# A two-layer decoder trunk on one core: the mixers' elementwise work on VectorE alone, and two weight parts split before the experts' last sum

## The chip, the core and the metric

One core of one Trainium2 chip. The metric is the device time of one execution in microseconds (us), as the median of several runs. TensorE does the matrix products, VectorE (DVE), ScalarE (ACT) and GpSimd (POOL) the elementwise work, SyncE (SP) issues the transfers from HBM.

## The reference, cut to what matters

T = 256 tokens of width 1024, two layers. Each layer has a mixer (three attention-like branches beside each other) and a mixture of 32 experts. All is float32.

```python
for l in range(2):
    mod = silu(c) @ ada_w[l] + ada_b[l]            # conditioning: 6 vectors of 1024
    sh1, sc1, gt1, sh2, sc2, gt2 = split(mod, 6)
    h = rms_norm(x, norm1_g[l]) * (1 + sc1) + sh1
    proj = h @ w_in[l]                             # 1024 -> 3524 columns
    rq, rk = rope(rq), rope(rk); ya = retention(rq, rk, rv, rg)
    yb = causal softmax attention with a cumulative forget gate (fq, fk, fv, ff)
    yc = causal softmax attention, low-rank q and kv, rope on 64 columns
    gates = sigmoid(h @ gate_w[l] + gate_b[l])     # 3 x 1024
    merged = g0 * (ya @ branch_w[0]) + g1 * (yb @ branch_w[1]) + g2 * (yc @ branch_w[2])
    x = x + gt1 * (merged @ out_w[l])
    h = rms_norm(x, norm2_g[l]) * (1 + sc2) + sh2
    x = x + gt2 * experts(h)                       # top-2 of 8 experts in the top group of 4
return rms_norm(x, final_g)
```

## The kernel before, in words

**Products in three parts.** The big products of the mixers run on TensorE as three cheaper ones (`mm3`, `gemm_tok`, `gemm_feat`). Weight and activation are each split into a high part, a cast to the type fp32r, and a low part, which is what the cast left over; high x high, high x low and low x high are added up in PSUM. A weight comes from HBM in tiles of 1 MiB (SP's queue, a ring of 12 slots, L141), and is consumed in chunks of 128 x 512. `split_w` (L247) makes the two parts of one chunk: ScalarE the high part (L256), VectorE or GpSimd the low part (L258), in one of four buffers `ws0` to `ws3`. `pump` (L242) is called once per chunk by the running product and keeps three chunks ready; it chooses the engine for the low part by a pattern: GpSimd, GpSimd, VectorE in general (`LO`), always GpSimd while `self.quiet` is set (`LO_HEADS`), which is the time of the softmax heads. An input slot is given back to the ring after its last low part.

**What runs between the chunks.** A product of eight chunks yields after each, and `step` then lets the generators in `live` go on by one step each: the heads of the two softmax attentions (L647 on, with the scaling L664), the forget gates (L804 to L820), the retention (scaling L908), and `chain`, the conditioning. `chain` takes its weights through VectorE: L505 and L507 multiply-add a 128 x 512 piece onto `acc`; TensorE sums `acc` over partitions and L525 adds the bias. So the order on each engine is that of the program text as these generators interleave; no engine reorders its own queue.

**Rotations and sums of branches.** `rope` (L632) makes four products on VectorE (L640 to L643) and the two sums on GpSimd (L644, L645). After a branch's product, `merge` multiplies with the gate on VectorE (L1146), and for the second and third branch `add_up` (L1117) adds the result to `merged` on GpSimd (L1120, 16 in all); for the last branch `split_a` then splits the sum for the output product (L268 on ScalarE, L269 on VectorE).

**The experts and the seam.** The experts' products take the weights unsplit, in 16 pairs; their elementwise work is VectorE's and ScalarE's. At the end `finish(n)` (L1368) adds the experts' sum to the residual for each half of the columns: L1375 and L1376 on VectorE, then a square with a sum of it on ScalarE (L1377), which writes its squares to `yp[n][0]` (`yh`). For n = 1 it comes after `open_split`, which opens the four buffers of the next layer. The next layer begins with `head` (L954): the norm, four warming matmuls, transposes, and, in its second piece, `split(2)` (L1003) for the first two chunks, with the low parts on GpSimd.

Of the kernel before, what the change touches and what calls it, by code (L numbers as in the profile page):

```python
# [8 lines left out]
F32 = mybir.dt.float32  # L9
# [4 lines left out]
AF = mybir.ActivationFunctionType  # L14
ALU = mybir.AluOpType
# [29 lines left out]
A_HG, A_MORE, A_HIDT, A_OH = (4864, 5888), (0, 2048, 6912), 4096, (4608, 8960)  # L45
# [7 lines left out]
ADA_LAG, ADA_DELAY = 5, 2  # L53

ADA_PAUSE = 4

LO_HEADS, LO = (1,), (0, 1, 1)

WAIT_MLA, WAIT_FOX, WAIT_RET, WAIT_PT = 4, 4, 2, 1
SLOTS = 12  # L60
# [107 lines left out]
class Trunk:  # L168
# [72 lines left out]

    def pump(self):  # L242
        while self.stream and len(self.splits) < len(self.ws) - 1:
            pattern = LO_HEADS if self.quiet else LO
            self.split_w(self.nc.gpsimd if pattern[(self.wsi + 1) % len(pattern)] else self.nc.vector)

    def split_w(self, eng):  # L247


        key, i, n, last = self.stream.popleft()  # L250
        if key not in self.held:
            self.held[key] = self.ring.take(key)
        w = self.held[key][1][:, i, :n]
        t = self.ws[self.wsi % len(self.ws)]
        hi, lo = t[:, 0, :n], t[:, 1, :n]
        self.nc.scalar.copy(hi, w)  # L256
        self.wsi += 1
        eng.tensor_tensor(lo, w, hi.bitcast(F32), ALU.subtract)  # L258
        self.splits.append((hi, lo))
        if last:  # L260
            self.ring.give(self.held.pop(key)[0])
# [370 lines left out]
    def rope(self, dst, src, t, heads):  # L632

        nc = self.nc
        b = self.v(A_ROPE, 2, heads, 32)
        c = self.cos[:, t][:, None, :].to_broadcast([P, heads, 32])
        s = self.sin[:, t][:, None, :].to_broadcast([P, heads, 32])
        x1, x2 = src[:, :, 0:32], src[:, :, 32:64]
        d1, d2 = dst[:, :, 0:32], dst[:, :, 32:64]
        nc.vector.tensor_tensor(b[:, 0], x2, s, ALU.mult)  # L640
        nc.vector.tensor_tensor(b[:, 1], x1, s, ALU.mult)
        nc.vector.tensor_tensor(d1, x1, c, ALU.mult)
        nc.vector.tensor_tensor(d2, x2, c, ALU.mult)  # L643
        nc.gpsimd.tensor_tensor(d1, d1, b[:, 0], ALU.subtract)  # L644
        nc.gpsimd.tensor_tensor(d2, d2, b[:, 1], ALU.add)  # L645

    def softmax_head(self, i, h, scores, bias, val, yr):  # L647

# [305 lines left out]
    def head(self, l):  # L954

        nc = self.nc
        xn = self.v(A_XN, 2, D)
        S, G = self.GS[:, 0, 0], self.GS[:, 0, 1]
        rs = [self.small(1) for _ in range(NT)]
        live = [self.inv_rms(t, rs[t]) for t in range(NT)]  # L960
        while live:
            self.step(live)
        for t in range(NT):
            nc.vector.tensor_scalar(xn[:, t, :512], self.x[:, t, :512], rs[t], None, ALU.mult)
            nc.scalar.mul(xn[:, t, 512:], self.x[:, t, 512:], rs[t])
        yield "normed"
        todo = []
        for g in range(2):
            for t in range(NT):
                ps = self.bank("s" if len(todo) < 3 and l else "g")  # L970
                for i in range(4):
                    j = 4 * g + i
                    self.tr(ps[:, 128 * i:128 * i + 128], xn[:, t, 128 * j:128 * j + 128])
                todo.append((g, t, ps))
        yield
        h32 = [self.v(A_H32 + 512 * k, 4, 128) for k in range(4)]

        def scaled(k):
            g, t, ps = todo[k]
            for i in range(4):  # L980
                j = 4 * g + i
                o, p = h32[k][:, i], ps[:, 128 * i:128 * i + 128]
                if t == 0:
                    nc.vector.tensor_scalar(o, p, G[:, j:j + 1], S[:, j:j + 1], ALU.mult, ALU.add)
                else:
                    nc.scalar.activation(o, p, AF.Identity, bias=S[:, j:j + 1], scale=G[:, j:j + 1])
            self.free(ps)

        def part(k, i):
            return self.hr[k // 2][:, i, :, 128 * (k % 2):128 * (k % 2) + 128]  # L990

        def high(k):
            nc.scalar.copy(part(k, 0), h32[k])

        def low(k):
            nc.vector.tensor_tensor(part(k, 1), h32[k], part(k, 0).bitcast(F32), ALU.subtract)

        def split(n):
            for _ in range(n):
                self.split_w(nc.gpsimd)  # L1000

        if l:
            split(2)  # L1003
        scaled(0)
        scaled(1)
        high(0)
        high(1)
        if l == 0:
            low(0)
            low(1)  # L1010
        yield
        if l == 0:
            split(2)
        scaled(2)
        if l:
            low(0)
            low(1)
        high(2)
        split(1)
        scaled(3)  # L1020
        low(2)
        high(3)
        low(3)
        split(1)

    def mixer(self, l):
        nc, run, finish = self.nc, self.run, self.finish
# [33 lines left out]
        ga = chain()  # L1061
        gh = self.heads.pop() if self.heads else self.head(l)
        if l:
            self.stream = deque(self.streams[l])
            next(gh)
            self.warm(4)
        self.together(gh)
# [46 lines left out]
        merged = self.v(A_MERGED, 8, 256)  # L1114
        sg = self.v(A_SG, 4, 256)

        def add_up(h, last):  # L1117
            for i in range(2):
                sl = slice(4 * h + 2 * i, 4 * h + 2 * i + 2)
                nc.gpsimd.tensor_tensor(merged[:, sl], merged[:, sl], sg[:, 2 * i:2 * i + 2], ALU.add)  # L1120
                yield
            for i in range(2 if last else 0):
                sl = slice(4 * h + 2 * i, 4 * h + 2 * i + 2)
                m = self.yr[1] if h == 0 else self.hr[0]
                self.split_a(m[:, 0, 2 * i:2 * i + 2], m[:, 1, 2 * i:2 * i + 2], merged[:, sl])
                yield
# [201 lines left out]
    def moe(self, l):  # L1328
        nc, tc = self.nc, self.tc
# [39 lines left out]
        def finish(n):  # L1369

            ns = slice(512 * n, 512 * n + 512)
            for t in range(NT):
                xs, ps = self.x[:, t, ns], self.sums[t][n]
                self.mm(ps, self.OT[:, 128 * t:128 * t + 128].bitcast(F32), y32[:, ns], False, True)
                nc.vector.tensor_tensor(hid, ps, self.gtb[:, ns], ALU.mult)  # L1375
                nc.vector.tensor_tensor(xs, xs, hid, ALU.add)  # L1376
                nc.scalar.activation(self.yp[n][0], xs, AF.Square, accum_out=self.ss[:, t, n:n + 1])  # L1377

        self.together(self.gather([self.v(A_OH[t], 2 * CAP) for t in range(NT)], hg[0], True))
        for p in range(NE // 2):  # L1380
# [242 lines left out]
```

## Time and profile before

| | |
|---|---|
| median of 3 runs | 1565.86 us (1561.02 to 1565.95) |
| the profiled execution | 1567.71 us, its span 1566.0 us |
| mixers, layer 0 and layer 1 | 0 to 335 us and 800 to 1095 us |
| experts, layer 0 and layer 1 | 335 to 800 us and 1095 us to the end |
| matmuls busy (PE) | 1488.0 us, 95% of the span |
| VectorE (DVE) | 641.0 us, 41% |
| ScalarE (ACT) | 449.8 us, 29% |
| GpSimd (POOL) | 336.6 us, 21%; 331.5 us of it in the mixers |
| mean granted TensorE clock | 0.973 |
| DMA | 342 GB/s over the span |

A share over the whole span mixes two kinds of stage. In the experts from 335 to 800 us VectorE is busy 103.9 us and GpSimd not at all; in the mixer from 0 to 335 they are busy 234.9 and 167.4 us. What matters in each stage is therefore read from views of that stage, and from the view that says for whom TensorE waited.

### The profile page before, as it was taken

Reading aid. Unit: us, or ns where it says so; the run is one execution under the profiler, and the core shown is the slowest. Engines: PE = TensorE matmul, PEld = TensorE weight load, DVE = VectorE, ACT = ScalarE, POOL = GpSimd, SP = SyncE. Lnnn points to the kernel's source line nnn. Section 1 sums busy time; section 2 is a strip of 40 time slices with the busy share of each in tenths; the row PEclk is TensorE's granted clock in tenths of the full one; section 3 lists DMA queues with packets and bytes.
Section 4 is the critical chain, followed back from the end, with each engine's and each line's share of the span. In section 5 each row is a group of like instructions: output and inputs, shape, how many; then the busy total and the mean of one; then the engine's idle time right before and its main releaser. Section 6 shows DMA issues by size and latency. Waiting matters only on the chain. (4 is left out here: it accounts for less than half of the span.)

```text
span 1566.0 us, 21356 instructions
## 1 busy us (share of the span) xinstructions
PE 1488.0 (95%) x8342; PEld 915.1 (58%) x8342; DVE 641.0 (41%) x1500; ACT 449.8 (29%) x896; POOL 336.6 (21%) x266
## 2 busy tenths in 40 slices
PE   6999999899999999999989999999999999999996
PEld 3877888654444444444458788896444444444442
DVE  3846878861222222122147559656222122222223
ACT  3555434331211111111154563353211111111111
POOL 1557546510000000000024664473000000000001
PEclk9899989899999999999999999999999999999998
DMA  9963676788999999999985646568899999999992
GB/s 385 367 236 135 231 280 243 295 348 361 421 421 421 420 421 421 421 419 421 410 336 188 228 176 251 209 230 314 353 421 421 420 421 422 421 420 419 421 416 108
DMA packets 78542, 535.16 MB, mean 342 GB/s; under 512 B 8608, under 2 KB 8864, under 8 KB 15968
## 3 DMA queue, kind: packets, MB, share of 16 engines
q1 hardware_dynamic: 77776, 532.89, 84.1%
q8 instruction: 69, 1.13, 0.3%
q10 hardware_dynamic: 656, 0.80, 0.1%
q14 instruction: 41, 0.34, 0.1%
HBM read 532.61 MB, written 1.05 MB: 341 GB/s over the span
## 5 line engine op out<-in xcount | busy, mean ns | idle before, releaser
L181 PE MATMUL bank<-slot,ar 128*64 128x512 f32 (+1 forms) x1880 | 491.4, 595 | 3.8 <-issue 1.6
L258 POOL TENSOR_TENSOR ws<-slot,ws 128x512 fp32r<-128x512 f32 (+1 forms) x209 | 284.4, 1372 | 711.8 <-ACT ws L256 693.6
L181 PEld LDWEIGHTS bank<-slot,ar 128*64 128x64 f32 (+1 forms) x1880 | 152.8, 138 | 276.8 <-issue 256.0
L256 ACT CAST ws<-slot 128x512 fp32r<-128x512 f32 (+1 forms) x276 | 169.3, 618 | 168.1 <-PE bank L181 154.3
L181 PE MATMUL bank<-hr,ws 128*128 128x256 f32 x1536 | 209.5, 296 | 7.7 <-POOL ws L258 6.7
L181 PE MATMUL bank<-ar 128*64 128x512 f32 (+3 forms) x692 | 209.3, 503 | 0.0
L181 PEld LDWEIGHTS bank<-hr,ws 128*128 128x128 f32 x1536 | 198.7, 201 | 13.7 <-POOL ws L258 7.3
L181 PE MATMUL bank<-ws,hr 128*128 128x512 f32 (+1 forms) x576 | 153.8, 413 | 9.1 <-DVE hr L269 4.3
L1325 ACT ACTIVATE ar<-bank,GS 128x128 f32<-128x128 f32 x128 | 58.5, 457 | 357.3 <-PE bank L181 326.6
L181 PE MATMUL bank<-more_left,ar 128*64 128x512 f32 x456 | 137.6, 595 | 0.0
L181 PEld LDWEIGHTS bank<-ar,x 128*128 128x128 f32 x1024 | 119.3, 192 | 25.1 <-issue 21.1
L507 DVE SCALAR_TENSOR_TENSOR acc<-slot,cz,acc 128x512 f32<-128x512 f32 x122 | 133.2, 1092 | 1.6
L181 PE MATMUL bank<-ar,x 128*128 128x128 f32 x1024 | 128.3, 279 | 1.8 <-DVE ar L1307 1.6
L181 PEld LDWEIGHTS bank<-ws,hr 128*128 128x128 f32 x576 | 108.7, 196 | 35.5 <-DVE hr L269 5.3
L1442 DVE SCALAR_TENSOR_TENSOR yl<-bank,wsl,yh 128x512 fp32r<-128x512 f32 x60 | 45.0, 751 | 157.1 <-ACT yh L1441 157.1
L181 PE MATMUL bank<-more_right,ar 128*64 128x512 f32 x308 | 106.4, 606 | 1.8 <-DMA more_left<-in_exp_w 1.8
L1359 DVE COPY wsl<-bank 64x1 f32<-64x1 f32 x64 | 10.0, 156 | 232.5 <-PE bank L181 232.1
L1560 POOL TENSOR_TENSOR ar<-x,cst 128x512 f32<-128x512 f32 x2 | 2.6, 1287 | 473.5 <-DVE x L1376 473.5
L1323 DVE TENSOR_SCALAR ar<-bank,GS 128x128 f32<-128x128 f32 x128 | 52.5, 410 | 116.3 <-ACT ar L1325 116.3
L258 DVE TENSOR_TENSOR ws<-slot,ws 128x512 fp32r<-128x512 f32 (+1 forms) x67 | 66.7, 997 | 70.8 <-ACT ws L256 65.4
L181 PEld LDWEIGHTS bank<-ar 128*64 128x64 f32 (+2 forms) x692 | 81.1, 155 | 24.6 <-issue 18.1
L1406 DVE TENSOR_TENSOR R<-R,bank 128x512 f32<-128x512 f32 x32 | 22.0, 687 | 178.4 <-PE bank L181 178.4
(244 smaller groups left out, 1362.2 us busy)
## 6 DMA issues: line engine op xcount, KB each, us to landing
slot<-in_exp_w SPq DMA_DIRECT2D x227, 1024.0 KB, 19.6
ar<-in_exp_w SPq DMA_DIRECT2D x54, 1024.0 KB, 19.8
more_left<-in_exp_w SPq DMA_DIRECT2D x54, 1024.0 KB, 19.8
slot<-in_ada_w SPq DMA_DIRECT2D x46, 1024.0 KB, 6.8
more_right<-in_exp_w SPq DMA_DIRECT2D x37, 1024.0 KB, 19.0
slot<-in_w_in SPq DMA_DIRECT2D x24, 1024.0 KB, 6.9
slot<-in_gate_w SPq DMA_DIRECT2D x23, 1024.0 KB, 5.3
slot<-in_branch_w SPq DMA_DIRECT2D x12, 1024.0 KB, 4.8
```

Of the source, the lines that this page charges most:

```text
L181: self.nc.tensor.matmul(out, lhsT, rhs, start=start, stop=stop, skip_group_check=True)
L256: self.nc.scalar.copy(hi, w)
L258: eng.tensor_tensor(lo, w, hi.bitcast(F32), ALU.subtract)
L507: nc.vector.scalar_tensor_tensor(acc, v[:, t, :], c, acc, ALU.mult, ALU.add)
L1323: nc.vector.tensor_scalar(hgT[:, j], pv[:, i], G[:, j:j + 1], S[:, j:j + 1], ALU.mult, ALU.add)
L1325: nc.scalar.activation(hgT[:, j], pv[:, i], AF.Identity, bias=S[:, j:j + 1], scale=G[:, j:j + 1])
L1359: nc.vector.tensor_copy(wsl(p)[es], ps[es, 256 + e:257 + e])
L1406: nc.vector.tensor_tensor(hid, hid, G[1], ALU.mult)
L1442: nc.vector.scalar_tensor_tensor(self.yp[n][1], G[n], wsl(p), self.yp[n][0].bitcast(F32), ALU.mult, ALU.subtract)
L1560: nc.gpsimd.tensor_tensor(y[:, t, ns], self.x[:, t, ns], self.fg[n], ALU.mult)
```

## The change

All low parts of the weights (L258), the two sums of the rotation (L644, L645) and the sums of the branches (L1120) go from GpSimd to VectorE. The pattern goes. At the seam the list of the next layer's chunks is set before `finish(1)`, and the first two chunks are split there instead of in `head`; since `yh` lies in the space that the new buffers then use, the squares of n = 1 go to a scratch in `ar` (`A_HIDT`).

```diff
-LO_HEADS, LO = (1,), (0, 1, 1)
...
     def pump(self):
         while self.stream and len(self.splits) < len(self.ws) - 1:
-            pattern = LO_HEADS if self.quiet else LO
-            self.split_w(self.nc.gpsimd if pattern[(self.wsi + 1) % len(pattern)] else self.nc.vector)
+            self.split_w()
...
-        eng.tensor_tensor(lo, w, hi.bitcast(F32), ALU.subtract)
+        self.nc.vector.tensor_tensor(lo, w, hi.bitcast(F32), ALU.subtract)
...
-        nc.gpsimd.tensor_tensor(d1, d1, b[:, 0], ALU.subtract)
-        nc.gpsimd.tensor_tensor(d2, d2, b[:, 1], ALU.add)
+        nc.vector.tensor_tensor(d1, d1, b[:, 0], ALU.subtract)
+        nc.vector.tensor_tensor(d2, d2, b[:, 1], ALU.add)
...
-        if l:
-            split(2)
         scaled(0)
...
         if l:
-            self.stream = deque(self.streams[l])
             next(gh)
...
-                nc.gpsimd.tensor_tensor(merged[:, sl], merged[:, sl], sg[:, 2 * i:2 * i + 2], ALU.add)
+                nc.vector.tensor_tensor(merged[:, sl], merged[:, sl], sg[:, 2 * i:2 * i + 2], ALU.add)
...
-                nc.scalar.activation(self.yp[n][0], xs, AF.Square, accum_out=self.ss[:, t, n:n + 1])
+                nc.scalar.activation(self.v(A_HIDT, 512) if n else self.yp[n][0], xs, AF.Square, accum_out=self.ss[:, t, n:n + 1])
...
         if l + 1 < DEPTH:
             self.open_split(l + 1)
+            self.stream = deque(self.streams[l + 1])
+            self.split_w()
+            self.split_w()
         finish(1)
```

TensorE's and SP's instructions keep their order, ScalarE's change at the seam alone, GpSimd's queue loses 256 instructions and VectorE's gains them. Behind the cuts the changed kernel's lines have smaller numbers: L258 is L255 there, L507 is L504, L269 is L266, L640 to L645 are L637 to L642, L1120 is L1114, L1146 is L1140, L1375 and L1376 are L1369 and L1370. `ws_0_135` to `ws_0_138` are the four buffers of layer 0, `slot_N` the ring's slots.

GpSimd's queue near 60 us, where the first rotations of layer 0 stand (`slot_91` and `slot_93` hold weights of w_in), before:

```order
L258 TENSOR_TENSOR ws_0_135<-slot_91,ws_0_135 128x512
L258 TENSOR_TENSOR ws_0_136<-slot_91,ws_0_136 128x512
L644 TENSOR_TENSOR ar<-ar 128x32
L645 TENSOR_TENSOR ar<-ar 128x32
L644 TENSOR_TENSOR ar<-ar 128x32
L645 TENSOR_TENSOR ar<-ar 128x32
L258 TENSOR_TENSOR ws_0_138<-slot_91,ws_0_138 128x512
L258 TENSOR_TENSOR ws_0_135<-slot_93,ws_0_135 128x512
L258 TENSOR_TENSOR ws_0_137<-slot_93,ws_0_137 128x512
```

And VectorE's queue at the same place now:

```order
L637 TENSOR_TENSOR ar<-ar,sin 128x32
L638 TENSOR_TENSOR ar<-ar,sin 128x32
L639 TENSOR_TENSOR ar<-ar,cos 128x32
L640 TENSOR_TENSOR ar<-ar,cos 128x32
L641 TENSOR_TENSOR ar<-ar 128x32
L642 TENSOR_TENSOR ar<-ar 128x32
L711 COPY ar<-ar 128x64
L810 TENSOR_SCALAR sm<-lfx 128x8
L811 TENSOR_TENSOR lfx<-sm 128x8
L255 TENSOR_TENSOR ws_0_138<-slot_91,ws_0_138 128x512
L504 SCALAR_TENSOR_TENSOR acc<-slot_92,cz,acc 128x512
```

The low part of `slot_91` in `ws_0_138` stood behind four half rotations of 128 x 32 on an engine that had nothing else; it stands now behind the same rotations, a copy and two steps of the forget gate (L810, L811) in the queue of the engine that makes them.

VectorE's queue at the last merge of layer 0, near 300 us (`ar` is the arena that holds `merged` and `sg`, `hr` takes the low part of the output product's activation), before:

```order
L507 SCALAR_TENSOR_TENSOR acc<-slot_92,cz,acc 128x512 x3
L1146 TENSOR_TENSOR ar<-bank_63,ar 128x512
L1146 TENSOR_TENSOR ar<-bank_64,ar 128x512
L258 TENSOR_TENSOR ws_0_138<-slot_89,ws_0_138 128x512
L507 SCALAR_TENSOR_TENSOR acc<-ar,cz,acc 128x512 x3
L269 TENSOR_TENSOR hr_0_139<-ar,hr_0_139 128x512
L258 TENSOR_TENSOR ws_0_137<-slot_90,ws_0_137 128x512
L507 SCALAR_TENSOR_TENSOR acc<-ar,cz,acc 128x512
L269 TENSOR_TENSOR hr_0_139<-ar,hr_0_139 128x512
```

And now:

```order
L1140 TENSOR_TENSOR ar<-bank_63,ar 128x512
L1140 TENSOR_TENSOR ar<-bank_64,ar 128x512
L255 TENSOR_TENSOR ws_0_138<-slot_89,ws_0_138 128x512
L504 SCALAR_TENSOR_TENSOR acc<-ar,cz,acc 128x512
L1114 TENSOR_TENSOR ar<-ar 128x512
L255 TENSOR_TENSOR ws_0_135<-slot_90,ws_0_135 128x512
L504 SCALAR_TENSOR_TENSOR acc<-ar,cz,acc 128x512
L1114 TENSOR_TENSOR ar<-ar 128x512
L255 TENSOR_TENSOR ws_0_136<-slot_90,ws_0_136 128x512
L504 SCALAR_TENSOR_TENSOR acc<-ar,cz,acc 128x512
L266 TENSOR_TENSOR hr_0_139<-ar,hr_0_139 128x512
L255 TENSOR_TENSOR ws_0_137<-slot_90,ws_0_137 128x512
L504 SCALAR_TENSOR_TENSOR acc<-ar,cz,acc 128x512
L266 TENSOR_TENSOR hr_0_139<-ar,hr_0_139 128x512
```

Two sums of the branches (L1114) and two more low parts (L255) stand now ahead of the first and the second low part of the sum (L266); the products, multiply-adds and splits keep their order among themselves.

VectorE's queue at the seam, before (the last sums of the experts, then the two pairs of L1375 and L1376 for each half of the columns):

```order
L1406 TENSOR_TENSOR R<-R,bank_64 128x512
L1375 TENSOR_TENSOR R<-bank_65,ar 128x512
L1376 TENSOR_TENSOR x<-x,R 128x512
L1375 TENSOR_TENSOR R<-bank_67,ar 128x512
L1376 TENSOR_TENSOR x<-x,R 128x512
L1375 TENSOR_TENSOR R<-bank_66,ar 128x512
L1376 TENSOR_TENSOR x<-x,R 128x512
L1375 TENSOR_TENSOR R<-bank_68,ar 128x512
L1376 TENSOR_TENSOR x<-x,R 128x512
```

And now:

```order
L1400 TENSOR_TENSOR R<-R,bank_64 128x512
L1369 TENSOR_TENSOR R<-bank_65,ar 128x512
L1370 TENSOR_TENSOR x<-x,R 128x512
L1369 TENSOR_TENSOR R<-bank_67,ar 128x512
L1370 TENSOR_TENSOR x<-x,R 128x512
L255 TENSOR_TENSOR ws_1_4940<-slot_94,ws_1_4940 128x452
L255 TENSOR_TENSOR ws_1_4941<-slot_94,ws_1_4941 128x452
L1369 TENSOR_TENSOR R<-bank_66,ar 128x512
L1370 TENSOR_TENSOR x<-x,R 128x512
L1369 TENSOR_TENSOR R<-bank_68,ar 128x512
L1370 TENSOR_TENSOR x<-x,R 128x512
```

The two low parts of the next layer's first chunks (128 x 452) stand between the first half's sums and the second half's.

## Rows read from the trace of the kernel before

**Rows 1.** The view of waits, engine PE (TensorE), whole run. Columns: engine, tile and line of the instruction that waited, what it waited for (engine, tile and line), us in total, times, longest wait. Lines in order of their sums, those that end in an instruction of another kind left out.
```profile
PE bank L181 <- POOL ws L258: 10.8, 8, 2.8
...
PE bank L190 <- DVE ar L908: 4.7, 6, 1.5
PE bank L181 <- DVE hr L269: 4.3, 1, 4.3
PE bank L181 <- DVE ws L258: 4.1, 5, 1.9
...
PE bank L181 <- DVE R L525: 3.6, 2, 1.8
...
PE bank L190 <- DVE ar L664: 2.3, 4, 1.0
...
PE bank L181 <- DVE acc L507: 2.0, 2, 1.7
```

**Rows 2.** The view of windows: busy time of each engine in five stretches of the mixers. Columns: the stretch in us from the span's start, its length, then for PE, PEld (weight loads), DVE (VectorE), ACT (ScalarE) and POOL (GpSimd) busy us and the number of instructions, the granted TensorE clock (1.00 is 2.4 GHz, 0.50 is 1.2 GHz), the share of the DMA engines' time in use, GB/s.
```profile
40.00:80.00 40.00, 36.23 (x231) 34.18 (x230) 33.71 (x71) 20.67 (x43) 21.27 (x22) 0.89 0.91 368
80.00:180.00 100.00, 97.54 (x583) 83.21 (x584) 57.14 (x112) 55.50 (x123) 62.36 (x49) 1.00 0.52 198
180.00:231.00 51.00, 46.84 (x328) 42.74 (x327) 43.59 (x93) 18.11 (x33) 23.80 (x18) 0.90 0.65 249
240.00:303.00 63.00, 54.14 (x388) 49.84 (x387) 61.93 (x52) 27.73 (x51) 45.31 (x30) 0.96 0.75 289
940.00:1000.00 60.00, 55.85 (x405) 51.14 (x404) 54.46 (x111) 21.54 (x39) 29.43 (x22) 0.92 0.64 245
```

**Rows 3.** The timeline of PE at three places. Columns: start us, length us, engine, line, operation, tiles out<-in with shapes, how many instructions are drawn together, and in brackets how long the engine had been idle before and what ended that.
```profile
62.83 2.50 PE L181 MATMUL bank<-hr,ws 128*128 128x256 f32 x10 [2.77 <-POOL ws L258]
...
199.99 3.13 PE L181 MATMUL bank<-hr,ws 128*128 128x256 f32 x24
...
302.62 2.08 PE L181 MATMUL bank<-ws,hr 128*128 128x512 f32 x4 [4.33 <-DVE hr L269]
```

**Rows 4.** The timeline of VectorE and GpSimd at two places, from 288.86 (both engines) and from 302.49 (VectorE, GpSimd idle). Columns as in Rows 3.
```profile
288.86 4.45 DVE L507 SCALAR_TENSOR_TENSOR acc<-slot,cz,acc 128x512 f32<-128x512 f32 x3
...
288.86 1.27 POOL L258 TENSOR_TENSOR ws<-slot,ws 128x512 fp32r<-128x512 f32 x1 [2.91 <-ACT ws L256]
291.48 1.29 POOL L258 TENSOR_TENSOR ws<-slot,ws 128x512 fp32r<-128x512 f32 x1 [1.34 <-ACT ws L256]
...
302.49 0.68 DVE L258 TENSOR_TENSOR ws<-slot,ws 128x512 fp32r<-128x512 f32 x1
303.09 0.74 DVE L507 SCALAR_TENSOR_TENSOR acc<-ar,cz,acc 128x512 f32<-128x512 f32 x1
303.75 0.68 DVE L269 TENSOR_TENSOR hr<-ar,hr 128x512 fp32r<-128x512 f32 x1
```

**Rows 5.** The view of groups of instructions, VectorE from 240 to 303 us, shapes apart. Columns: line, engine, operation, tiles, out<-in shapes, count | busy us, mean ns of one | idle time just before them.
```profile
L507 DVE SCALAR_TENSOR_TENSOR acc<-slot,cz,acc 128x512 f32<-128x512 f32 x24 | 32.7, 1364 | 0.5
L258 DVE TENSOR_TENSOR ws<-slot,ws 128x512 fp32r<-128x512 f32 x10 | 12.3, 1229 | 5.6 <-ACT ws L256 5.6
L507 DVE SCALAR_TENSOR_TENSOR acc<-ar,cz,acc 128x512 f32<-128x512 f32 x3 | 5.1, 1691 | 0.1
```

**Rows 6.** The view of one source line, L258 (the low part), GpSimd's instructions of it. Columns: line, engine, operation, tiles, count: shortest/median/longest duration in ns, first and last start, shapes.
```profile
L258 POOL TENSOR_TENSOR ws<-slot,ws x209: 1142/1292/1830, 34.7 to 1063.2; 128x512 fp32r<-128x512 f32 x97, 128x452 fp32r<-128x452 f32 x8
```

**Rows 7.** The timeline of GpSimd and VectorE before the matmul of 62.83 us. Columns as in Rows 3.
```profile
61.51 3.73 POOL L258 TENSOR_TENSOR ws<-slot,ws 128x512 fp32r<-128x512 f32 x3
...
52.35 1.24 DVE L807 TENSOR_TENSOR sm<-lfx,sm 128x8 f32<-128x8 f32 x1
...
55.12 1.86 DVE L507 SCALAR_TENSOR_TENSOR acc<-slot,cz,acc 128x512 f32<-128x512 f32 x1
```

**Rows 8.** The view of groups, VectorE from 180 to 231 us. Columns as in Rows 5.
```profile
L507 DVE SCALAR_TENSOR_TENSOR acc<-slot,cz,acc 128x512 f32<-128x512 f32 x14 | 13.3, 953 | 0.1
L258 DVE TENSOR_TENSOR ws<-slot,ws 128x512 fp32r<-128x512 f32 x8 | 7.3, 911 | 0.0
L908 DVE TENSOR_SCALAR ar<-ar,sm 128x128 f32<-128x128 f32 x8 | 4.2, 527 | 0.3
...
L900 DVE TENSOR_TENSOR sm<-sm,cst 128x4 f32<-128x4 f32 x2 | 1.4, 704 | 0.0
```

**Rows 9.** The timeline of ScalarE and VectorE at the seam of the layers. Columns as in Rows 3.
```profile
796.18 0.67 ACT L1439 ACTIVATE ar<-bank,wsl 128x512 f32<-128x512 f32 x1
...
799.52 0.63 ACT L1377 ACTIVATE yh<-x 128x512 fp32r<-128x512 f32 x1 [2.67 <-DVE x L1376]
...
805.13 1.02 ACT L256 CAST ws<-slot 128x452 fp32r<-128x452 f32 x2
...
798.07 0.69 DVE L1375 TENSOR_TENSOR R<-bank,ar 128x512 f32<-128x512 f32 x1 [2.61 <-PE bank L181]
```

**Rows 10.** Four single rows on the transfers: the view of waits for SP's queue (columns as in Rows 1), the view of windows for a stretch of the experts (columns as in Rows 2), and the timeline of ScalarE at two successive pairs of experts (columns as in Rows 3).
```profile
SPq L141 <- POOL ws L258: 228.0, 43, 18.9
...
400.00:500.00 100.00, 100.00 (x518) 45.26 (x516) 22.03 (x67) 14.11 (x26) 0.00 (x0) 1.00 1.01 421
...
575.01 0.60 ACT L1402 ACTIVATE R<-bank 128x512 f32<-128x512 f32 x1 [6.26 <-PE bank L181]
...
602.86 0.60 ACT L1402 ACTIVATE R<-bank 128x512 f32<-128x512 f32 x1 [6.26 <-PE bank L181]
```

More of the change, by code (lines that the diff above doesn't have):

```diff
@@ L243, in pump, with split_w @@
         while self.stream and len(self.splits) < len(self.ws) - 1:
-            pattern = LO_HEADS if self.quiet else LO
-            self.split_w(self.nc.gpsimd if pattern[(self.wsi + 1) % len(pattern)] else self.nc.vector)
-    def split_w(self, eng):
+            self.split_w()
+    def split_w(self):
         key, i, n, last = self.stream.popleft()
@@ L999, in split @@
             for _ in range(n):
-                self.split_w(nc.gpsimd)
-        if l:
-            split(2)
+                self.split_w()
         scaled(0)
@@ L1446, in moe @@
             self.open_split(l + 1)
+            self.stream = deque(self.streams[l + 1])
+            self.split_w()
+            self.split_w()
         finish(1)
```

## Prediction, made before the changed kernel was run

> **What bounds the kernel now.** Read first who made TensorE wait [rows 1]. Matmuls fill 95% of the span, so the time is TensorE's own work plus its waits, and a change to VectorE and GpSimd can move the time only through those waits, and through what a wait does to TensorE's clock. Seven rows of that view name an instruction that this change moves, or one that stands in a queue with such a one; together they are 10.8 + 4.7 + 4.3 + 4.1 + 3.6 + 2.3 + 2.0 = 31.8 us. Then the stages [rows 2]: the column PEclk says where the clock was halved. A stage of 51 us at 0.90 spent 51 x 0.10 x 2 = 10.2 us at 1.2 GHz instead of 2.4, and lost half of that, 5.1 us. Where TensorE had waited, as at 62.8 and 302.6 [rows 3], the stages read 0.89 and 0.96; from 80 to 180, where it hardly waits, 1.00.
>
> Why are the parts late? In the stage from 240 to 303 VectorE is busy 61.9 of 63 us and GpSimd 45.3 [rows 2]. But VectorE is slow there rather than loaded. [Rows 4] show three multiply-adds (L507) that took 4.45 us with two GpSimd subtractions of 1.27 and 1.29 us beside them; with GpSimd idle, a subtraction and a multiply-add take VectorE 0.60 and 0.66 us from start to next start (302.49, 303.09, 303.75). So each GpSimd instruction takes about its own length from VectorE: 4.45 - 3 x 0.66 = 2.5 us for 2.56 us of GpSimd. In that stage the mean L507 is 1.364 us and the mean subtraction (L258) 1.229 us [rows 5].
>
> **The change, part by part.** *Removed from GpSimd:* 216 low parts at 1.29 us in the median [rows 6], 16 sums of the branches and 24 halves of the rotations. *Added to VectorE:* the same, at 0.60 us each for 512 columns [rows 4], less for a half rotation. In the stage 240 to 303 all 30 of GpSimd's instructions [rows 2] have 512 columns, 30 x 0.60 = 18.0 us. What VectorE has there already costs, alone, 27 x 0.66 + 12 x 0.60 for the L507 and L258 [rows 5] (two L258 in it work from `ar`), and some 7.5 us for 13 others, 32.5 us. Sum 50.5 us. TensorE's own work in the stage is 54.1 us [rows 2], less about 2.6 us given back by the clock, 51.5 us. The two are nearly level, so I let the stage fall from 63 to about 53 us and not to 51.
>
> The waits, one by one, with what replaces them:
> - GpSimd's low parts, 10.8 us in 8 waits [rows 1]. Two of 2.8 us (62.8 and its twin in layer 1) come from GpSimd's queue: the low part stands behind two rotations that wait for VectorE [rows 3, 7]. On VectorE it stands behind the same rotations and two steps of the forget gate. VectorE gains about 1.1 us each on L807 and L507 there [rows 7] and an estimated 2 us on shorter ones, and takes on three subtractions, four half rotations and the late one itself, about 3.4 us. I book 0.5 us for each, and leave the halved clock behind them as it is. The other six, 5.2 us, go: low parts that need 0.60 us instead of 1.29, in a queue without the rotations' wait. Together 6.2 us.
> - VectorE's own low parts, 4.1 us, and the last sums' low part (hr L269), 4.3 us. The latter is waited for at 302.6 [rows 3] behind three L507 of 1.69 us each [rows 5] and two GpSimd sums. Alone, two products, two sums, two low parts and what stands between them fit into some 6 us, where TensorE has four chunks of 1.56 us (two in 3.13 us [rows 3]). I book 7.0 of 8.4 us.
> - L507 as releaser, 2.0 us, and the softmax scaling L664, 2.3 us, slowed in the same way: 4.0 of 4.3 us.
> - The retention's scaling L908, 4.7 us, and the conditioning sum L525, 3.6 us, in the stages from 180 and 940. Here VectorE is not relieved: of 43.6 us, [rows 8] give back 14 x 0.20 + 8 x 0.22 + 8 x 0.24 + 2 x 0.53 = 7.5 us against the same operations alone, the shorter ones an estimated 4 us more, and 18 moved instructions bring 10.8 us. I book half, 4.2 us.
> - The clock. From 180 and from 940 the halved time is 10.2 and 9.6 us [rows 2], a loss of 9.9 us; I book 4.5 us, as half of the waits before them go. From 240 to 308 two halved stretches lose 5.1 us, of which I book 2.5 us. Together 7.0 us.
> - The two low parts made ahead at the seam of the layers. Their casts fall into ScalarE's idle 2.67 us before 799.52 and cost nothing there; without that idle time they would cost 1.0 us. The subtractions start behind casts of 0.51 us from 796.85 on, and the residual sum that started at 798.07 now stands behind them [rows 9]: with two at 0.60 us it starts near 798.7. The chain behind it slips by 0.6 us, and nothing comes back, since ScalarE waited for TensorE after the casts' old place. Loss 0.6 us. The square's other scratch costs nothing: same size, same engine.
> - Queues. GpSimd's has nothing left that waits, and none of the mixers' transfers are issued there. SP's and TensorE's rows keep their order. SP waits for freed slots, and these come free as TensorE and VectorE get on, hence earlier.
>
> Sum: 6.2 + 7.0 + 4.0 + 4.2 + 7.0 - 0.6 = 27.8 us. The profiled execution took 1567.7 us, so **1540 us**. The median of the runs is 1565.9, 1.8 us below it, the lowest 1561.0; I stay with the sum against the profiled one. The ceiling, every wait of the seven rows and all the clock behind them (9.9 + 5.1 + 6.8 for 62.8 and its twin), is 53.6 us, 1514 us.
>
> A rule goes against the budget of [rows 2, 5]. The Trainium skill's page "Perfetto Trace Analysis", in "Optimizing Scalar/DVE Operations", holds that with VectorE saturated, giving some work to ScalarE or even GpSimd may make sense. By it, the third rival below, the sum would be a loss of 35 us. The same section warns that the two engines share a read port, so that this may not help, and of the two halves the trace agrees with the second.
>
> **The rivals.**
> *VectorE becomes the bound in the full stages.* In one queue, a low part waits for whatever stands ahead of it, and the budgets above are level (50.5 against 51.5; 43.6 + 10.8 - 11.5). Then the bookings for L908, L525 and the clock are lost, half of the second and 2.0 us of the first: 16.7 us, leaving 11.1 us, 1557 us. For it: VectorE had 1.1 us of idle in 63. Against: a low part is made three chunks ahead.
> *The transfers take it back.* In the experts' stage the DMA engines move 421 GB/s without a break [rows 10], a 1 MiB tile in 2.49 us, 29.9 us for the 12 of a pair of experts, while TensorE needs 27.85 us (575.01 to 602.86). The lead shrinks by 2 us a pair. If the first tiles do not come earlier, an estimated 12 us are paid at the ends: 1552 us. Against: SP waits 228 us for low parts of GpSimd's to free slots [rows 10], and those waits shrink.
> *The slow times are VectorE's own.* If L507 keeps 1.36 us without GpSimd, the moved instructions go on top [rows 2], at 0.60 us: 61.9 + 18.0 in 63, 33.7 + 13.2 in 40, 43.6 + 10.8 in 51, 54.5 + 13.2 in 60, or 16.9 + 6.9 + 3.4 + 7.7 = 35 us more, 1603 us. It decides if less than 17 of the 61.9 us come back in the first of them; I count on 29. [Rows 4] speak against it.
> *Low parts behind softmax steps that wait.* **Slower.** From 80 to 180, and in layer 1 alike, nearly all low parts are GpSimd's (49 instructions [rows 2]), and TensorE hardly waits. On VectorE such a part can stand behind a step that itself waits for ScalarE or TensorE. If 90 chunks of both layers lose 0.55 us each, 50 us, the time is 1568 - 28 + 50 = 1590 us. It turns to a loss from 0.31 us a chunk. Against: a softmax step and a low part take an estimated 1.5 us together, three chunks of lead are 4.7 us.
> *The change gives nothing,* because the waits move to the casts: 1566 us. *All of it goes:* 1514 us.
>
> **How the numbers follow.** Forecast, 1524 to 1555: 0.62. First rival 0.14, second 0.05, third 0.03, fourth 0.06, nothing 0.05, all 0.05. A measurement of this kernel tells about 0.3% from no change, 4.7 us, so faster is below 1561: 0.62 + 0.13 + 0.05 + 0.05 = 0.85. Same: 0.06 (nothing, and the edge of the first rival). Slower: 0.09. The range 1520 to 1560 leaves out the two slower rivals, the null and the ceiling, 0.19.
>
> **What would show it.** Right: L507 and L258 near 0.7 us in every stage; no wait of matmuls on low parts but two behind the rotations, near 60 and 830; hr L269 below 1 us; the stage that was 240 to 303 about 10 us shorter, its clock at 0.98 or more; each pair of experts still 27.85 us. Wrong: new waits of matmuls on VectorE's low parts between 80 and 180 (fourth rival), L507 above 1 us (third), or waits for expert tiles late in a layer (second).

## The result

| | before | changed |
|---|---|---|
| median of the runs | 1565.9 us (1561.02 to 1569.1, 4 runs) | 1548.36 us (1547.08 to 1554.6, 4 runs) |
| ratio | | 0.9887, 95% interval 0.9868 to 0.9906 |
| profiled execution, span | 1567.71 us, 1566.0 us | 1547.87 us, 1546.2 us |

The change gains 17.5 us (1.1%), where 25.9 us from the median, or 27.8 us from the profiled execution, were forecast. The time lies in the range of 1520 to 1560 us, and it is shorter than before, as forecast. That the sum came as near as it did is partly luck: between the two profiled executions two of its terms were wrong by more than 9 us each, with opposite signs.

### The profile page after: what moved, and what is told of

The parts are those of the page before. It is cut to its first block, busy times and chain, and to the rows that moved or that the text cites. A ratio compares the mean times of both kernels' runs of the same rounds, so it can differ in the third digit from the quotient of the medians.

```text
span 1546.2 us, 21291 instructions
## 1 busy us (share of the span) xinstructions
PE 1471.1 (95%) x8342; PEld 902.8 (58%) x8342; DVE 662.3 (43%) x1756; ACT 449.8 (29%) x896; POOL 5.9 (0%) x10
## 5 line engine op out<-in xcount | busy, mean ns | idle before, releaser
L255 DVE TENSOR_TENSOR ws<-slot,ws 128x512 fp32r<-128x512 f32 (+1 forms) x276 | 188.2, 686 | 99.2 <-ACT ws L253 90.6
L253 ACT CAST ws<-slot 128x512 fp32r<-128x512 f32 (+1 forms) x276 | 168.3, 617 | 138.0 <-PE bank L179 121.6
L179 PE MATMUL bank<-hr,ws 128*128 128x256 f32 x1536 | 203.1, 290 | 3.6 <-DVE ws L255 3.6
L179 PEld LDWEIGHTS bank<-hr,ws 128*128 128x128 f32 x1536 | 193.1, 195 | 8.9 <-DVE ws L255 4.0
L504 DVE SCALAR_TENSOR_TENSOR acc<-slot,cz,acc 128x512 f32<-128x512 f32 x122 | 91.4, 749 | 0.0
L179 PEld LDWEIGHTS bank<-more_left,ar 128*64 128x64 f32 x456 | 41.0, 137 | 82.5 <-issue 76.6
L1435 ACT ACTIVATE yh<-bank,wsl 128x512 fp32r<-128x512 f32 x60 | 41.2, 687 | 150.7 <-PE bank L179 150.7
## 6 DMA issues: line engine op xcount, KB each, us to landing
slot<-in_exp_w SPq DMA_DIRECT2D x227, 1024.0 KB, 19.8
ar<-in_exp_w SPq DMA_DIRECT2D x54, 1024.0 KB, 19.8
more_left<-in_exp_w SPq DMA_DIRECT2D x54, 1024.0 KB, 19.8
```

The costliest lines, as they stand in the source:

```text
L179: self.nc.tensor.matmul(out, lhsT, rhs, start=start, stop=stop, skip_group_check=True)
L255: self.nc.vector.tensor_tensor(lo, w, hi.bitcast(F32), ALU.subtract)
L504: nc.vector.scalar_tensor_tensor(acc, v[:, t, :], c, acc, ALU.mult, ALU.add)
L1435: nc.scalar.mul(self.yp[n][0], G[n], wsl(p))
```

## The profile after

The page's first part of the changed kernel, busy us (share of the span) and instructions of each engine:

```profile
PE 1471.1 (95%) x8342; PEld 902.8 (58%) x8342; DVE 662.3 (43%) x1756; ACT 449.8 (29%) x896; POOL 5.9 (0%) x10
```

The 8342 matmuls take 1488.0 - 1471.1 = 16.9 us less, and no matmul was changed: that is clock (mean granted 0.973 before, 0.984 now; 1566.0 x 0.027 = 42 us lost to it before, 1546.2 x 0.016 = 25 us now). The rest of the span, which TensorE waits, fell from 78.0 to 75.1 us only. VectorE has 256 instructions more, 232 of them of about 512 columns, which at 0.60 us would be 139 us, and 21.3 us more of busy time: the others got shorter.

This split into clock and waits is that of two single executions, and the granted clock differs between runs of one kernel. The 27 runs of the kernel before that were made beside the experiments have 0.973 to 0.980, the median 0.977, and the profiled one stands at the lower end; three of the changed kernel's four have 0.984, one 0.977. By the medians the same sum gives 36 us before and 25 us now, an estimate of 11 us of clock and some 6 us of waits in the 17.5 us gained.

For whom TensorE waits, columns as in [rows 1]; L661 is the softmax scaling (L664 before), L255 the low parts, L879 a step of the retention's scores, L522 and L266 the former L525 and L269:

```profile
PE bank L188 <- DVE ar L661: 14.9, 10, 2.4
...
PE bank L179 <- DVE ws L255: 5.1, 7, 1.8
...
PE bank L188 <- DVE ar L961: 4.4, 1, 4.4
...
PE bank L179 <- DVE ar L879: 3.3, 2, 1.7
PE bank L179 <- DVE R L522: 2.6, 2, 1.3
...
PE bank L179 <- DVE hr L266: 1.5, 1, 1.5
...
PE bank L179 <- ACT ws L253: 1.1, 2, 0.7
```

Against [rows 1]: the low parts of both engines went from 10.8 + 4.1 to 5.1 us, the last sums' low part from 4.3 to 1.5, L908 and L507 are gone. But the softmax scaling went from 2.3 us in 4 waits to 14.9 us in 10.

The stages of [rows 2] again, each from the same matmul to the same matmul (both kernels have the same matmuls in the same order, so they can be matched one by one):

```profile
39.30:77.10 37.80, 34.58 (x229) 32.41 (x230) 31.52 (x93) 22.70 (x48) 0.00 (x0) 0.95 0.97 396
77.10:184.90 107.80, 100.27 (x583) 84.16 (x584) 72.63 (x164) 55.68 (x123) 0.00 (x0) 0.98 0.50 185
184.90:230.20 45.30, 42.37 (x327) 39.59 (x324) 41.54 (x110) 18.01 (x33) 0.00 (x0) 0.96 0.72 267
239.30:290.60 51.30, 49.84 (x387) 47.48 (x385) 49.27 (x80) 27.56 (x51) 0.00 (x0) 1.00 0.84 319
928.10:983.20 55.10, 52.09 (x406) 48.53 (x405) 51.28 (x133) 21.50 (x39) 0.00 (x0) 0.97 0.70 262
```

The stretch from 240 fell from 63.0 to 51.3 us, the retention's from 51.0 to 45.3 and from 60.0 to 55.1. The stretch from 80, the softmax heads', *rose* from 100.0 to 107.8, with VectorE at 67%. Over the program the matched matmuls show the changed kernel 2.9 us ahead of before at 80 us, 4.9 us behind at 180 and 15.5 us ahead at the experts; in layer 1 it again loses 7.5 us in the heads (19.4 to 11.9 us ahead), and is 20.0 us ahead in the experts.

In the stretch that answers to [rows 5] VectorE's instructions have their undisturbed lengths:

```profile
L255 DVE TENSOR_TENSOR ws<-slot,ws 128x512 fp32r<-128x512 f32 x30 | 20.7, 691 | 1.3 <-ACT ws L253 1.2
L504 DVE SCALAR_TENSOR_TENSOR acc<-slot,cz,acc 128x512 f32<-128x512 f32 x24 | 18.0, 751 | 0.0
...
L504 DVE SCALAR_TENSOR_TENSOR acc<-ar,cz,acc 128x512 f32<-128x512 f32 x3 | 2.3, 751 | 0.0
```

L507's means of 1364 and 1691 ns became 751 ns, the low part's 1229 became 691. And the matmul that waited 4.33 us [rows 3], with the one at 62.83:

```profile
290.62 2.56 PE L179 MATMUL bank<-ws,hr 128*128 128x512 f32 x10 [1.48 <-DVE hr L266]
...
61.33 1.46 PE L179 MATMUL bank<-hr,ws 128*128 128x256 f32 x10 [1.78 <-DVE ws L255]
```

The loss in the heads is read from one place, VectorE, then ScalarE, then TensorE (L844 adds the bias to a head's scores, L655 finds the maximum, L656 is the exponential, L253 the cast of a chunk):

```profile
131.04 0.61 DVE L655 TENSOR_REDUCE sm<-ar 128x1 f32<-128x128 f32 x2
132.89 0.69 DVE L255 TENSOR_TENSOR ws<-slot,ws 128x512 fp32r<-128x512 f32 x1 [1.24 <-ACT ws L253]
133.50 0.55 DVE L844 SCALAR_TENSOR_TENSOR ar<-bank,ar 128x384 f32<-128x384 f32 x1
134.09 0.61 DVE L655 TENSOR_REDUCE sm<-ar 128x1 f32<-128x128 f32 x2
135.94 0.69 DVE L255 TENSOR_TENSOR ws<-slot,ws 128x512 fp32r<-128x512 f32 x1 [1.24 <-ACT ws L253]
136.55 0.74 DVE L504 SCALAR_TENSOR_TENSOR acc<-slot,cz,acc 128x512 f32<-128x512 f32 x1
137.21 0.15 DVE L659 RECIPROCAL sm<-sm 128x2 f32<-128x2 f32 x1
137.40 0.55 DVE L661 TENSOR_SCALAR ar<-ar,sm 128x128 f32<-128x128 f32 x2
...
131.36 0.40 ACT L656 ACTIVATE ar<-ar,sm 128x128 f32<-128x128 f32 x1 [2.42 <-DVE sm L655]
...
131.76 0.49 ACT L656 ACTIVATE ar<-ar,sm 128x256 f32<-128x256 f32 x1
...
132.26 0.60 ACT L253 CAST ws<-slot 128x512 fp32r<-128x512 f32 x1
134.41 0.40 ACT L656 ACTIVATE ar<-ar,sm 128x128 f32<-128x128 f32 x1 [1.55 <-DVE sm L655]
...
137.74 0.95 PE L188 MATMUL bank<-cst,ar 128*128 128x128 f32 x3 [2.44 <-DVE ar L661]
```

The cast at 132.26 stands on ScalarE behind a head's two exponentials, these wait for the maximum, and VectorE's low part of that chunk waits 1.24 us for the cast. Nobody needs this low part yet: in the view of waits from 77 to 185 us no matmul waits for a low part. But behind it on VectorE stands the next head's L844 of 133.50, whose scores are there; its exponentials and the next cast follow, the next low part waits 1.24 us again, and at the end TensorE waits 2.44 us for L661. Before, GpSimd's queue took that wait (33.2 us for casts from 80 to 180 us).

## The experiments

All of them were run beside runs of the kernel before (medians 1566.43 to 1566.66 us; the first line of the table is from the comparison above). PE busy and the rest of the span are those of the one profiled execution, so they shift with its clock, as said above. Theories and rivals with a number belong to the expectations of these experiments; the prediction's own rivals are called first to fourth.

| kernel | median us (runs) | ratio to before, 95% | span | PE busy | rest |
|---|---|---|---|---|---|
| before | 1565.9 (4) | | 1566.0 | 1488.0 | 78.0 |
| changed | 1548.36 (4) | 0.9887 (0.9868 to 0.9906) | 1546.2 | 1471.1 | 75.1 |
| e1_heads_gpsimd | 1530.8 (5) | 0.9768 (0.9745 to 0.979) | 1529.1 | 1466.0 | 63.1 |
| e2_before_heads_vector | 1586.73 (4) | 1.0123 (1.0105 to 1.014) | 1586.6 | 1494.7 | 91.9 |
| e3_low_one_later | 1528.56 (5) | 0.9765 (0.9741 to 0.9788) | 1523.9 | 1463.9 | 60.0 |
| e3b_all_one_later | 1524.81 (5) | 0.9719 (0.9699 to 0.9739) | 1523.7 | 1462.3 | 61.4 |
| e4_idle_gpsimd | 1614.61 (1) | | 1612.6 | 1497.6 | 115.0 |
| f1_lows_only | 1539.64 (5) | 0.9824 (0.9806 to 0.9843) | 1537.9 | 1471.8 | 66.1 |
| f2_sums_only | 1554.25 (6) | 0.9916 (0.99 to 0.9932) | 1550.3 | 1471.7 | 78.6 |
| f3_no_seam | 1548.25 (4) | 0.9885 (0.9863 to 0.9907) | 1545.4 | 1471.2 | 74.2 |
| f5_warm_in_wait | 1577.06 (1) | | 1575.4 | 1491.4 | 84.0 |

**The heads: order or load.** Three kernels on the low parts of the softmax heads' stage. e1_heads_gpsimd gives them back to GpSimd:

```diff
-        self.nc.vector.tensor_tensor(lo, w, hi.bitcast(F32), ALU.subtract)
+        eng = self.nc.gpsimd if self.quiet else self.nc.vector
+        eng.tensor_tensor(lo, w, hi.bitcast(F32), ALU.subtract)
```

> The changed kernel, but in the stage of the softmax heads GpSimd makes the low parts, as before. Theory 1 (on VectorE a low part waits there for a cast that stands behind the heads' exponentials, and holds up the next head's steps; matched matmul by matmul, that stage got 7.9 us longer in layer 0 and 7.5 in layer 1): 15 us less than the changed kernel, 1533 us (1528 to 1538), the waits on the softmax scaling back from 14.9 us to about 2.3. Rival 1 (GpSimd's instructions slow VectorE there by as much as the casts' order costs, or the waits only move): 1543 to 1550 us.

Measured 1530.8 us, and the waits on the softmax scaling (L662 there) as before:

```profile
PE bank L188 <- DVE ar L662: 2.3, 4, 1.0
```

GpSimd lengthens VectorE's instructions there too, the multiply-add to 930 ns and the scaling to 952, where the changed kernel has 747 and 287 from 77 to 185 us (VectorE from 75 to 165 us, columns as in [rows 5]; then the windows' row from 73 us). It costs little, as VectorE has room, 53.8 us busy in 90:

```profile
L505 DVE SCALAR_TENSOR_TENSOR acc<-slot,cz,acc 128x512 f32<-128x512 f32 x13 | 12.1, 930 | 0.0
...
L662 DVE TENSOR_SCALAR ar<-ar,sm 128x128 f32<-128x128 f32 x8 | 7.6, 952 | 0.3
...
73.00:163.00 90.00, 88.86 (x508) 75.04 (x507) 53.77 (x110) 52.20 (x116) 43.21 (x33) 1.00 0.54 200
```

e2_before_heads_vector moves the low parts of the heads' stage to VectorE, and nothing else, in the kernel before:

```diff
-LO_HEADS, LO = (1,), (0, 1, 1)
+LO_HEADS, LO = (0,), (0, 1, 1)
```

> The kernel before, and only the low parts of the softmax heads' stage go to VectorE. Theory 1: slower than before by about 15 us, 1581 us (1576 to 1587), with the waits on the softmax scaling at 12 to 15 us instead of 2.3. Rival 1: within 5 us of before, 1561 to 1571 us.

Measured 1586.73 us, 20 us slower, 5 more than expected, and 16.2 us of waits where 12 to 15 were:

```profile
PE bank L190 <- DVE ar L664: 16.2, 10, 3.1
```

Of the 20.6 us that its profiled span is longer, 13.9 are waits and 6.7 clock.

e3_low_one_later keeps everything on VectorE and changes the order alone: in this stage `split_w` first issues the low part of the chunk before, whose cast is older than the heads' last exponentials.

```diff
     def split_w(self):
+        self.low_w()
...
-        self.nc.vector.tensor_tensor(lo, w, hi.bitcast(F32), ALU.subtract)
+        self.late = (lo, w, hi, key if last else None)
+        if not self.quiet:
+            self.low_w()
         self.splits.append((hi, lo))
-        if last:
-            self.ring.give(self.held.pop(key)[0])
```

(`low_w` issues the waiting low part and gives its slot back; `next_w` calls it if that chunk is the one needed.)

> The changed kernel, all on VectorE, but in the softmax heads' stage a chunk's low part is issued one chunk later than its cast, so that it never stands ahead of a head's steps with its cast still to come. Theory 1 (it is the order, not VectorE's load): 1531 us (1526 to 1537), the waits on the softmax scaling below 4 us. Rival 2 (VectorE's load in that stage, with the moved instructions, delays the heads whatever the order): 1543 to 1549 us, waits of 12 to 15 us.

Measured 1528.56 us; the view of waits has no line for the scaling (L673 there) at all. The same place as above, VectorE:

```profile
127.76 0.61 DVE L667 TENSOR_REDUCE sm<-ar 128x1 f32<-128x128 f32 x2
128.28 0.68 DVE L248 TENSOR_TENSOR ws<-slot,ws 128x512 fp32r<-128x512 f32 x1
128.88 0.55 DVE L856 SCALAR_TENSOR_TENSOR ar<-bank,ar 128x384 f32<-128x384 f32 x1
129.47 0.61 DVE L667 TENSOR_REDUCE sm<-ar 128x1 f32<-128x128 f32 x2
130.00 0.68 DVE L248 TENSOR_TENSOR ws<-slot,ws 128x512 fp32r<-128x512 f32 x1
130.60 0.75 DVE L516 SCALAR_TENSOR_TENSOR acc<-slot,cz,acc 128x512 f32<-128x512 f32 x1
131.26 0.16 DVE L671 RECIPROCAL sm<-sm 128x2 f32<-128x2 f32 x1
131.46 0.55 DVE L673 TENSOR_SCALAR ar<-ar,sm 128x128 f32<-128x128 f32 x2
```

And the windows' row of 90 us in this stage:

```profile
73.00:163.00 90.00, 89.30 (x511) 75.50 (x510) 62.12 (x144) 52.52 (x117) 0.00 (x0) 1.00 0.53 200
```

From the first maximum to L673 (127.76 to 131.46) it takes 3.7 us, where the changed kernel took 6.4 (131.04 to 137.40): the two waits of 1.24 us are gone. VectorE does as much as in the changed kernel, and TensorE is busy 89.3 of 90 us. Matched, the stage that was 80 to 180 takes 98.5 us, 99.0 in e1_heads_gpsimd and 108.1 in the changed kernel. So it was the order, not the load; rival 2 is out.

e3b_all_one_later does it everywhere:

```diff
         self.late = (lo, w, hi, key if last else None)
-        if not self.quiet:
-            self.low_w()
```

> As the kernel with each low part one chunk later than its cast, but everywhere and not only in the heads' stage. Theory 1 (a low part should never stand ahead of other steps while its cast is still to come): the 6.4 us of VectorE's waits for casts near 225 to 290 go, but few matmuls wait for it there: 1527 us (1521 to 1532). Rival 5 (three chunks of lead are needed outside the heads): 1533 us or more, with the waits on the low parts above 10 us.

Measured 1524.81 us, the fastest, within theory 1's range. But the waits on low parts rose to 12.5 us in 14, as rival 5 had it, while others fell, and PE busy is the lowest. That it beats e3_low_one_later is not settled: they ran beside different runs of before, and the intervals lie end to end (0.9741 and 0.9739).

**What GpSimd costs VectorE.** e4_idle_gpsimd loads GpSimd with work that nothing reads (a second line, which sets `quiet`, keeps it off the two splits at the seam):

```diff
         self.nc.vector.tensor_tensor(lo, w, hi.bitcast(F32), ALU.subtract)
+        if self.attended and not self.quiet and self.wsi % 3:
+            for k in range(0, 512, 256):
+                self.nc.gpsimd.tensor_tensor(self.v(8960, 256), w[:, k:k + 256], hi[:, k:k + 256].bitcast(F32), ALU.subtract)
```

> The changed kernel, and behind two of three low parts in the stage of the gates and branches (after the softmax heads) GpSimd also makes a low part, in two halves of 256 columns, into a scratch that nothing reads. Theory 2 (a GpSimd instruction takes about its own length from VectorE): L504 there again above 1.2 us in the mean instead of about 0.7, and the time 1575 to 1640 us, as VectorE then bounds that stage. Rival 3 (VectorE's long instructions were its own, GpSimd cost only by its low parts coming late): L504 unchanged, 1546 to 1552 us.

Measured 1614.61 us. VectorE and GpSimd in one stretch (L507 is L504 of the changed kernel, L1143 a product that reads PSUM):

```profile
261.98 1.22 DVE L507 SCALAR_TENSOR_TENSOR acc<-slot,cz,acc 128x512 f32<-128x512 f32 x1
263.12 1.22 DVE L255 TENSOR_TENSOR ws<-slot,ws 128x512 fp32r<-128x512 f32 x1
264.27 1.21 DVE L507 SCALAR_TENSOR_TENSOR acc<-slot,cz,acc 128x512 f32<-128x512 f32 x1
...
267.69 0.68 DVE L1143 TENSOR_TENSOR ar<-bank,ar 128x512 f32<-128x512 f32 x1
...
261.59 6.78 POOL L258 TENSOR_TENSOR ar<-slot,ws 128x256 f32<-128x256 f32 x6
```

And VectorE's group from 240 to 320 us:

```profile
L507 DVE SCALAR_TENSOR_TENSOR acc<-slot,cz,acc 128x512 f32<-128x512 f32 x24 | 26.0, 1081 | 0.0
```

GpSimd's six take 6.78 us, one every 1.14 us, of 1.07 us in the median; VectorE's start every 1.14 us too, instead of every 0.60 or 0.66: one of each in turn. The product from PSUM keeps 0.68 us. The mean of L507, 1081 ns, is less than the 1.2 us that was expected, since GpSimd was busy 57 of the 70 us from 250 and not all of them; rival 3 (751 ns, 1546 to 1552 us) is out. The Trainium skill's page "SBUF — State Buffer", in "Who interferes with whom", says that a VectorE instruction with two inputs in SBUF contends with a GpSimd instruction that reads SBUF, that the shared ports are an exclusive lock, and that a VectorE instruction with at most one input there contends only in its two-port modes. The rows of L507, L255 and L1143 agree; whether the scaling of e1_heads_gpsimd (one input, 952 ns) runs in such a mode no row shows. Where VectorE was full (61.9 of 63 us) GpSimd's work had to go; where it had room (e1_heads_gpsimd, 53.8 of 90 us) it did no harm that the time shows (1530.8 us against 1528.56 of e3_low_one_later). Of the two halves of what the prediction weighed from the Trainium skill's page "Perfetto Trace Analysis", in "Optimizing Scalar/DVE Operations", the advice that GpSimd may take over some of a saturated VectorE's work did not pay here, and the warning of the shared read port held (a multiply-add of 1364 ns beside GpSimd took 751 without it).

**Which moves brought it.** Two kernels made from the one before. First f1_lows_only, the low parts outside the heads' stage, then f2_sums_only, the rotations' sums (and, by the same word, those of the branches in `add_up`):

```diff
-LO_HEADS, LO = (1,), (0, 1, 1)
+LO_HEADS, LO = (1,), (0,)
...
-                self.split_w(nc.gpsimd)
+                self.split_w(nc.vector)
```

```diff
-        nc.gpsimd.tensor_tensor(d1, d1, b[:, 0], ALU.subtract)
-        nc.gpsimd.tensor_tensor(d2, d2, b[:, 1], ALU.add)
+        nc.vector.tensor_tensor(d1, d1, b[:, 0], ALU.subtract)
+        nc.vector.tensor_tensor(d2, d2, b[:, 1], ALU.add)
```

> The kernel before, and only the low parts outside the softmax heads' stage go to VectorE; those of the heads, the rotations' sums and the branches' sums stay on GpSimd, the seam stays. Theory 2 (GpSimd's instructions lengthen VectorE's, and some 130 of the 190 that run beside a busy VectorE are these): most of the 36 us that the changed kernel with the heads on GpSimd gained, 1541 us (1534 to 1548). Rival 4 (the few sums that stand in waited chains are what counts): 1555 to 1566 us.

> The kernel before, and only the rotations' sums and the branches' sums go to VectorE, all low parts stay as they were. Theory 2: the two waits of 2.8 us behind the rotations go with the halved clock behind them, and some of the wait on the last sums' low part: 1556 us (1550 to 1562). Rival 4: 1530 to 1545 us.

Measured 27.0 and 12.4 us of gain, near what was expected; together 39.4, against 35.9 of e1_heads_gpsimd, which has both. Between the profiled executions 11.9 us of f1's gain are waits and 16.2 clock, and in f2 all is clock: 16.3 us, while waits rose by 0.6. By the runs' median clocks (0.977 before, 0.984 and 0.983) the clock's part is an estimated 11 of f1's 27.0 us and 10 of f2's 12.4. In f2 the low parts of GpSimd's fell to 3.2 us and the last sums' to 1.1 (and 1.3 for the high part), but a new wait stands behind the rotations, for the forget gate (L814):

```profile
PE bank L181 <- DVE lfx L814: 9.2, 2, 4.6
...
PE bank L181 <- POOL ws L258: 3.2, 6, 0.8
```

**The seam.** f3_no_seam leaves that part of the change out (the two splits stand in `head` again, and the squares go to `yh`):

```diff
             self.open_split(l + 1)
-            self.stream = deque(self.streams[l + 1])
-            self.split_w()
-            self.split_w()
         finish(1)
```

> The changed kernel without its part at the seam: the first two chunks of layer 1 are split in the head again (on VectorE), the squares of the second half go to yh again. By the prediction's step (the two low parts delay the residual sum by 0.6 us and nothing comes back): matched matmul by matmul against the changed kernel, layer 1's first products start 0.6 us earlier, and the time is 1547 us (1543 to 1551). Rival 7 (what they delay is given back at layer 1's first chunk, whose low part is ready): the norm's scaling is waited for 0.35 us less, the first products gain nothing or lose up to 1 us, 1549 us.

Measured 1548.25 us, the same as the changed kernel's 1548.36. Its wait for L961 is 4.07 us instead of 4.42. But matched, layer 1's first products (from 802 us) come 1.6 us later than in the changed kernel, with the clock at 0.74 instead of 0.91 in the 20 us from 784. The two programs are the same up to the seam, and there the executions already differ by about as much (1.5 us at 300 us). By the end it is gone (spans 1545.4 and 1546.2 us), so neither price is told by the time.

**The clock as a second price of a wait.** f5_warm_in_wait:

```diff
+                    if (l, n, j) == (0, 0, 4):
+                        b = self.bank("s")
+                        for _ in range(8):
+                            self.mm(b[:, 0:256], self.ident, self.cst[:, 0:256], True, True)
+                        self.free(b)
                     wh, wl = self.next_w()
```

> The kernel before with eight more matmuls of 128 x 256, whose result nothing reads, ahead of the matmul that waits 4.33 us for the last sums' low part in layer 0. Theory 3 (the wait costs a second time, by the clock behind it): the wait ends where it ended, no stretch at 0.5 begins near 301, and the program behind it comes 3.4 us earlier against before. Rival 6 (the clock is halved by something else): the stretch of 6.8 us stays and nothing is gained.

The added matmuls fill TensorE from 300.2 to 303.8 us. What is left of the wait in this kernel, then the 7 us behind it, then those 7 us of the kernel before:

```profile
304.95 2.33 PE L181 MATMUL bank<-ws,hr 128*128 128x512 f32 x9 [0.69 <-DVE hr L269]
```

```profile
305.00:312.00 7.00, 7.00 (x30) 4.86 (x31) 4.77 (x8) 1.86 (x3) 2.46 (x2) 1.00 0.98 389
```

```profile
303.00:310.00 7.00, 7.00 (x20) 4.20 (x20) 3.30 (x6) 1.23 (x2) 1.28 (x1) 0.65 0.95 365
```

The clock stays at 1.00 instead of 0.65, and from the end of the wait until TensorE waits next, for L258 at 316, it takes 11.3 instead of 13.7 us. So 2.4 us of the 3.4 expected, as part of the halved stretch lay inside the wait; theory 3 holds at this place. The whole kernel got slower (one run), for reasons elsewhere that were not studied: two waits of 5.7 and 6.0 us in the experts, at the branch for overflowing experts (1.9 and 1.6 us in the kernel before).

## Why the prediction was right and where it was wrong

| term | booked | measured in the profiles |
|---|---|---|
| low parts of both engines, last sums | 6.2 + 7.0 | 10.8 + 4.1 + 4.3 to 5.1 + 1.5: 12.6 |
| L507 and the softmax scaling | 4.0 | 2.0 + 2.3 to 0 + 14.9: -10.6 |
| L908 and L525 | 4.2 | 4.7 + 3.6 to 0 + 2.6, and 3.3 new for L879: 2.4 |
| seam | -0.6 | -0.3 in the wait, nothing in the time |
| clock | 7.0 | 16.9 |
| other waits | 0 | -1.2 |
| sum | 27.8 | 19.8 |

*The mechanism* was right: VectorE was slow because of GpSimd. L507 fell to 751 ns, the full stage to 51.3 us where 53 were forecast, and e4 shows the price with nobody waiting. Its size, "about its own length from VectorE", holds in [rows 4]; in e4 a GpSimd instruction of 1.07 us takes 0.5 us.

*The signs* that the text named came true in the full stage (clock 1.00, 0.98 forecast; L504 0.75 us, 0.7 forecast; two waits left behind the rotations, of 1.8 us), but for the last sums' low part, 1.5 us instead of below 1, and five short waits on low parts, 1.5 us together, where none were forecast. New waits between 80 and 180, the sign of the fourth rival, came too, though on the softmax scaling and not on low parts, as that sign had it.

*The failed step* is the booking of the softmax scaling as one of the waits "slowed in the same way". It looked at what lengthens L664, and that did go (952 to 287 ns for 128 x 128); it did not look at what would stand ahead of it. The fourth rival had the place, the low parts in the heads, but the other way round, a low part behind a waiting softmax step, and argued it away with three chunks of lead: these protect the low part, which is indeed never late there, and not the softmax steps queued behind it. It isn't a rival, with a chance of 0.06, but a term: e1 and e3 put it at 17.6 and 19.8 us (1548.36 to 1530.8 and 1528.56). Its price was bounded too high (50 us): in layer 0's heads VectorE waits 26.6 us for casts (77 to 185 us), and only five waits, 7.5 us, reach TensorE.

*The mis-sized term* is the clock. I booked the halved time at three places and only half of it. PE busy fell by 16.9 us between the profiled executions, some 11 us by the runs' medians, and the ceiling in the text had 21.8. f5 shows at one place that a wait is paid again by the clock behind it. But how much clock goes with how much wait stays open. Of the 27 runs of the kernel before, nine at 0.973 lost 0.004 x 1566 = 6.3 us more to the clock than ten at 0.977, and took only 2.7 us longer in the median. The wait of 1.82 us for L525 tells the same. The windows of 20 us behind it, of the kernel before, f2_sums_only and f5_warm_in_wait in turn:

```profile
221.20:241.20 20.00, 19.94 (x127) 18.32 (x128) 6.30 (x15) 5.63 (x10) 7.59 (x6) 0.83 0.45 172
```

```profile
220.00:240.00 20.00, 19.95 (x140) 18.32 (x141) 8.72 (x17) 6.99 (x13) 6.22 (x5) 0.91 0.53 203
```

```profile
220.60:240.60 20.00, 19.94 (x101) 18.31 (x102) 5.30 (x13) 4.13 (x7) 5.37 (x5) 0.66 0.41 159
```

The clock is 0.83, 0.91 and 0.66 after the same wait. Up to there the first and the third are the same program, so 0.83 and 0.66 differ by the execution alone, and with that f5's matmuls fall 3.1 us back.

*The seam's* step was right in its wait (0.35 us for the 0.6 booked), and "nothing comes back" is open: the profiles show 1.6 us by 802 us, the other way, with a different clock, and about what two executions of one program differ by.

*The other rivals.* Transfers: the gain of 15.5 us at 358 us is still there at 797, and a pair of experts takes 27.85 us as before (559.57 to 587.42 at L1396). VectorE as the bound in the full stages: 49.3 of 51.3 us busy, nearly level as worked out, and TensorE waits there at most 1.5 us.

## What to carry to other kernels

Before you move an instruction into another in-order queue, ask two things: how late is it there, and what stands behind it while it waits for its own input? Lead protects the moved instruction alone; issuing it one step later, when its input is ready, gave here what moving it to another engine gave. And book a wait of TensorE as the wait plus the clock behind it, the second with a wide range; take it from the granted clocks of several runs, not from one profile.

## What was not expected of the hardware

A GpSimd subtraction of 128 x 256 took 1.07 us in the median beside a busy VectorE (0.73 us beside its product from PSUM), only a sixth less than one of 128 x 512 in the kernel before (1.29 us), its starts in turn with VectorE's. And the same wait of 1.82 us was followed by very different times at the half clock, in one and the same program too, as the three rows above show.
